# Down projections of a SwiGLU layer by seven products instead of eight, token differences on VectorE, h transposes one product later

## The chip, the cores and the metric

The kernel runs on one core of a Trainium2 chip. Its time is the device time of one execution in microseconds (us); lower is better. TensorE (PE) multiplies, VectorE (DVE), ScalarE (ACT) and GpSimd (POOL) work on vectors, and SyncE (SP) starts the transfers from HBM.

## The reference

One decoder layer in float32 for 256 tokens of width 2048. Each step works on an rms-normed x and is added to x:

```python
def swiglu(h, w_gate, w_up, w_down):
    return (jax.nn.silu(h @ w_gate) * (h @ w_up)) @ w_down

x = x + 0.5 * swiglu(rms_norm(x, ffn1_norm), ffn1_w_gate, ffn1_w_up, ffn1_w_down)
x = x + hybrid_mixer(...)        # attention and gated linear attention, 256 x 6160 and 2048 x 2048
x = x + cross_attention(...)     # 256 memory tokens, 4 heads of 128
x = x + 0.5 * swiglu(rms_norm(x, ffn2_norm), ffn2_w_gate, ffn2_w_up, ffn2_w_down)
```

w_gate and w_up are 2048 x 5632, w_down is 5632 x 2048. The change concerns the two ffns (swiglu) alone.

## The kernel before

**Precision.** Every f32 operand is split in two parts, hi and lo, and a product is three passes on TensorE: hi·wh, hi·wl, lo·wh. A weight tile `raw` (128 x 2048 f32, 512 rows of the weight by 512 columns, 1 MB) is loaded by SP's queue; `parts` cuts it in two halves, and for each ScalarE casts `wh` (L174) and VectorE subtracts `wl = raw - wh` (L175). wh and wl have four buffers each, so splitting can be four half tiles ahead of TensorE. `wgroup` does the same for ordinary projections (L127, L128).

**Stages of an ffn.** The 5632 hidden columns are 11 chunks f of 512, in two segments (0 to 5, 6 to 10). For each f the kernel computes gate and up (x times a 512-column chunk of w_gate and of w_up, accumulated over four groups of 512 rows of x), `silu` of gate on ScalarE (L366), times up on VectorE (L372, the rows `s<-s,r,sg`), which gives h for two token halves. The h chunk is transposed by TensorE (`turn`, four 128x128 transposes for each token half, L343) and split into `hTh` and `hTl` (L262 for the latter). After a segment, its h chunks are multiplied with w_down, 512 columns c at a time (c from 0 to 3), and x is updated (L379).

**Seven products.** For f > 0 `seven` computes gate and up of a chunk together. Its first two row groups make a 2 x 2 block problem: token half 1 and 2 of x by row group 1 and 2 (blocks A11, A12, A21, A22), row group by gate or up column (b11, b21, b12, b22). Seven block products stand for eight: weights are added (`add` on VectorE, L180, into b11 in place: b11+b21, then +b12, then +b22; a fourth sum on POOL's accumulating transfer, `add_hbm`), and x differences (`F`, five of them) take the place of x blocks. One block product (`product`) is 12 matmuls of 128x512 on a PSUM bank. The other row groups are ordinary (`plain`, 24 matmuls a tile). Four PSUM banks Y, Z, X, R hold the sums; Y is copied twice on ScalarE on the way (`s21`, `s22`) before it grows on. The products come in this order:

1. Y = A21·(b11+b21); ScalarE copies Y to s21
2. Z = F22-21·b21
3. Y += F12-21·(b11+b21+b12); ScalarE copies Y to s22
4. X = F22-12·b22
5. R = A12·(b11+b21+b12+b22)
6. Y += F21-11·b12; later the plain tiles, and last Y += F11-12·(b12+b11)

**Differences.** `differences()` runs once for each ffn, ahead of the first seven: four sums xf = xTh + xTl and five d on POOL, five `Fh` on ScalarE, five `Fl` on VectorE (L221). At the kernel's start POOL also makes the packed products of x and gain (L284) out of which xTh and xTl come.

**Order.** A scheduler sets the order on each engine from the order of the code and priorities: what stands in `tc.high_priority(WPRI)` (weights, their splits, `add`) goes ahead. `later(n, fn)` puts fn behind the n-th next `tick`, and every half tile of weights ticks once. So `later(1, ...)` puts the h transposes of one chunk near the middle of the first products of the next seven.

Of the kernel before, what the change touches and what calls it, by code (L numbers as in the profile page):

```python
# [38 lines left out]
XPRI = 170  # L39
MEM0 = 2  # L40
MEMS = 3
UB = 34
SB = 8
RB = 5
SEGS = (range(0, 6), range(6, NF))


@with_exitstack
def layer_kernel(ctx: ExitStack, tc: tile.TileContext, A: dict, out: bass.AP):
# [26 lines left out]
    def later(n, fn):  # L76
        pend.append([n, fn])
# [80 lines left out]

    def load(W, c, g):
        with tc.high_priority(WPRI):
            raw = wp.tile([P, 4, 512], F32, tag="raw", name="raw", bufs=RB)
            SY.dma_start(raw, W[c, g])
        return raw

    def parts(raw):
# [37 lines left out]
    def differences():  # L205

        x = {}
        for c in range(2):
            for t in range(TT):
                x[t, c] = U([P, 4, P], F32, "xf")  # L210
                hi, lo = (p[:, :, t * P:(t + 1) * P].bitcast(F32) for p in xT[c])
                G.tensor_tensor(x[t, c], hi, lo, op=ALU.add)
        r = {}
        for name, a, b in (("22-21", (1, 1), (1, 0)), ("12-21", (0, 1), (1, 0)), ("22-12", (1, 1), (0, 1)),
                           ("21-11", (1, 0), (0, 0)), ("11-12", (0, 0), (0, 1))):
            d = W2([P, 4, P], "d")
            G.tensor_tensor(d, x[a], x[b], op=ALU.subtract)
            hi = U([P, 4, P], F32R, "Fh")
            lo = U([P, 4, P], F32R, "Fl")
            SC.copy(hi, d)  # L220
            V.tensor_sub(lo, d, hi.bitcast(F32))  # L221
            r[name] = (hi, lo)
        return r

    def seven(W1, W2_, f, F, A12, A21, rest):


        Y, Z, X, R = [pa.tile([P, 512], F32, tag="acc", name="acc") for _ in range(4)]
        b11 = load(W1, f, 0)
        b21 = load(W1, f, 1)  # L230
        add(b11, b21)
        product(Y, A21, b11, True)
        s21 = W2([P, 512], "s21")
        SC.copy(s21, Y)
        b12 = load(W2_, f, 0)
# [5 lines left out]
        b22 = load(W2_, f, 1)  # L241
        product(X, F["22-12"], b22, True)
        add(b11, b22)
        product(R, A12, b11, True)
        V.tensor_sub(s22, R, s22)
        product(Y, F["21-11"], b12, False)
        add_hbm(b12, W1[f, 0])
        s12 = W2([P, 512], "s12")
        SC.copy(s12, Y)
        for g in (2, 3):  # L250
            plain((R, X), (rest(0, g), rest(1, g)), load(W2_, f, g), (False, False), (1, 0))
        V.tensor_sub(s12, R, s12)
        V.tensor_add(s22, X, s22)
        plain((Y, Z), (rest(0, 2), rest(1, 2)), load(W1, f, 2), (False, False), (1, 0))
        product(Y, F["11-12"], b12, False)
        plain((Y, Z), (rest(0, 3), rest(1, 3)), load(W1, f, 3), (False, False), (0, 1))
        V.tensor_add(s21, Z, s21)
        return Y, s21, s12, s22

    def split_from_psum(hi, lo, ps):  # L260
        SC.copy(hi, ps)
        V.tensor_sub(lo, ps, hi.bitcast(F32))  # L262
# [70 lines left out]
    def ffn(pre, r, after, fine=None, last=False):  # L333
        wg, wu, wd = (A[f"{pre}_w_{n}"] for n in ("gate", "up", "down"))
        hT = {}

        def turn(f, hs):
            for t in range(TT):
                hi = U([P, 4, P], F32R, "hTh")
                lo = U([P, 4, P], F32R, "hTl")  # L340
                tp = PM([P, 4, P], "tp")
                for j in range(4):
                    PE.transpose(tp[:, j], hs[t][:, j * P:(j + 1) * P], ident)  # L343
                split_from_psum(hi, lo, tp)
                hT[f, t] = (hi, lo)

        def x_block(t, c):
            return tuple(p[:, :, t * P:(t + 1) * P] for p in xT[c])

        def lhs_h(k, t):  # L350
            return tuple(p[:, k % 4] for p in hT[k // 4, t])

        for seg in SEGS:
            for f in seg:
                if f == 0:
                    acc = proj(wg, f, lhs_x, range(4), fine)
                    if callable(r):
                        r = r()
                    F = differences()
                else:  # L360
                    y, s21, s12, s22 = seven(wg, wu, f, F, x_block(0, 1), x_block(1, 0), x_block)
                    acc = [y, s21]
                sg = []
                for t in range(TT):
                    s = acc[t] if f and t else W2([P, 512], "sg")
                    SC.activation(s, acc[t], AF.Silu, scale=r[:, t:t + 1])  # L366
                    sg.append(s)
                acc = [s12, s22] if f else proj(wu, f, lhs_x, range(4))
                hs = []
                for t in range(TT):  # L370
                    h = acc[t] if f else W2([P, 512], "h")
                    V.scalar_tensor_tensor(h, acc[t], r[:, t:t + 1], sg[t], op0=ALU.mult, op1=ALU.mult)  # L372
                    hs.append(h)
                later(1, lambda f=f, hs=hs: turn(f, hs))
            final = seg is SEGS[-1]
            for c in range(NC):
                acc = proj(wd, c, lhs_h, seg, last=last and final and c == NC - 1)
                for t in range(TT):
                    V.scalar_tensor_tensor(xs[c][:, t], acc[t], 0.5, xs[c][:, t], op0=ALU.mult, op1=ALU.add)  # L379
                if final:  # L380
                    after(c)


    def head_scale(acc, r, r2, t, scale_in, sign, name):
# [18 lines left out]
        return r2  # L403


    mhalf = con.tile([P, P], F32, name="mhalf")
    V.memset(mhalf, -0.5)

    warm = ST(1, "warm")
    SC.activation(warm, mhalf[:, 0:1], AF.Silu)  # L410
    wps = PM([P, P], "wps")
    for i in range(WARM):
        PE.matmul(wps, mhalf, mhalf, start=True, stop=True)
    ident = con.tile([P, P], F32, name="ident")
    make_identity(nc, ident)

# [83 lines left out]
    q_turn = gated("q", 6)  # L500


    r2b = con.tile([P, TT, 32], F32, name="r2b")
    V.tensor_copy(r2b, r2.unsqueeze(2).broadcast_to([P, TT, 32]))
    gps = PM([32, S], "gps")
    for k in range(16):
# [500 lines left out]
```

## Time and profile before

| | |
|---|---|
| median of 3 runs | 1964.46 us (1963.1 to 1965.01) |
| the profiled execution | 1964.76 us, its span 1962.7 us |
| TensorE busy | 1933.6 us (99%) |
| VectorE busy | 1366.8 us (70%) |
| ScalarE busy | 1064.6 us (54%) |
| POOL busy | 110.6 us (6%) |
| granted TensorE clock, mean | 0.997 of full speed |
| HBM traffic | 395.24 MB, 201 GB/s |

In a row of groups, the columns are line, engine, operation, tiles (out<-in) with shapes and count, then busy us and mean ns, then idle time just before them and what ended it. In a timeline row they are start and duration in us, then the instruction, and in brackets the idle time ahead of it and its releaser. Matmuls overlap, so a matmul's duration is longer than the distance to the next; distances between starts tell the rate. PEld is the load of the stationary operand.

### The profile page before, as it was taken

Reading aid. Unit: us, or ns where it says so; the run is one execution under the profiler, and the core shown is the slowest. Engines: PE = TensorE matmul, PEld = TensorE weight load, DVE = VectorE, ACT = ScalarE, POOL = GpSimd, SP = SyncE. Lnnn points to the kernel's source line nnn. Section 1 sums busy time; section 2 is a strip of 40 time slices with the busy share of each in tenths; the row PEclk is TensorE's granted clock in tenths of the full one; section 3 lists DMA queues with packets and bytes.
Section 4 is the critical chain, followed back from the end, with each engine's and each line's share of the span. In section 5 each row is a group of like instructions: output and inputs, shape, how many; then the busy total and the mean of one; then the engine's idle time right before and its main releaser. Section 6 shows DMA issues by size and latency. Waiting matters only on the chain.

```text
span 1962.7 us, 22466 instructions
## 1 busy us (share of the span) xinstructions
PE 1933.6 (99%) x8760; PEld 1582.1 (81%) x8760; DVE 1366.8 (70%) x1388; ACT 1064.6 (54%) x1305; POOL 110.6 (6%) x99
## 2 busy tenths in 40 slices
PE   8899999999999999999999999999999999999999
PEld 6688788888778888878888889778778888877887
DVE  6788874578887554646775665878886457888643
ACT  5556653355665445544576545656665335666532
POOL 4100000000000000001221000300000000000000
PEclk9899999999999999999999999999999999999999
DMA  8466565556667554535466553556657555666652
GB/s 343 153 211 236 195 238 194 194 207 216 220 209 241 204 182 154 178 129 209 172 215 214 188 184 143 178 190 232 210 199 256 193 193 194 229 202 212 237 214 84
DMA packets 60566, 395.24 MB, mean 201 GB/s; under 512 B 6795, under 2 KB 7947, under 8 KB 14252
## 3 DMA queue, kind: packets, MB, share of 16 engines
q1 hardware_dynamic: 56428, 370.74, 51.6%
q0 software_dynamic: 2880, 20.97, 5.8%
q10 hardware_dynamic: 1152, 2.10, 0.3%
q8 instruction: 68, 1.11, 0.2%
q14 instruction: 38, 0.31, 0.0%
HBM read 391.69 MB, written 2.10 MB: 201 GB/s over the span
## 4 chain that ended last, share of the span: by engine, by line
PE 68%; DVE 20%; DMA 6%; issue 5%; ACT 1%; SPq 0%; DVEq 0%; ACTq 0%
PE acc L138 17%; PE acc L136 17%; PE acc L137 17%; DVE wl L175 13%; DMA raw<-in_ffn_w_gate_dram 6%; PE acc L191 5%; PE acc L190 5%; PE acc L189 5%; DVE raw L180 3%; DVE s L372 1%; ACT wh L174 1%; DVE hTl L262 1%; DVE wl L128 1%; PE tp L343 0%; PE tp L302 0%
## 5 line engine op out<-in xcount | busy, mean ns | idle before, releaser
L128 DVE TENSOR_TENSOR wl<-raw,wh 128x1024 fp32r<-128x1024 f32 (+1 forms) x370 | 459.4, 1246 | 367.8 <-ACT wh L127 365.4
L127 ACT CAST wh<-raw 128x1024 fp32r<-128x1024 f32 (+1 forms) x370 | 386.5, 1048 | 441.0 <-PE acc L138 400.6
L174 ACT CAST wh<-raw 128x1024 fp32r<-128x1024 f32 x440 | 457.8, 1053 | 308.8 <-PE acc L191 274.6
L175 DVE TENSOR_TENSOR wl<-raw,wh 128x1024 fp32r<-128x1024 f32 x440 | 522.2, 1223 | 94.1 <-ACT wh L174 91.0
L189 PE MATMUL acc<-wh,xTh 128*128 128x512 f32 x800 | 314.4, 393 | 3.5 <-ACT sg L366 2.3
L190 PE MATMUL acc<-wl,xTh 128*128 128x512 f32 x800 | 314.2, 393 | 1.5 <-DVE wl L175 0.8
L191 PE MATMUL acc<-wh,xTl 128*128 128x512 f32 x800 | 313.6, 392 | 0.0
L136 PE MATMUL acc<-wh,hTh 128*128 128x512 f32 x704 | 274.6, 390 | 0.0
L138 PE MATMUL acc<-wh,hTl 128*128 128x512 f32 x704 | 274.0, 389 | 0.0
L137 PE MATMUL acc<-wl,hTh 128*128 128x512 f32 x704 | 274.0, 389 | 0.0
L136 PE MATMUL acc<-wh,xTh 128*128 128x512 f32 x544 | 215.0, 396 | 5.4 <-ACT wh L127 2.8
L137 PE MATMUL acc<-wl,xTh 128*128 128x512 f32 x544 | 212.5, 391 | 2.6 <-DVE wl L128 2.6
L138 PE MATMUL acc<-wh,xTl 128*128 128x512 f32 x544 | 212.0, 390 | 0.7 <-DVE xTl L286 0.7
L189 PEld LDWEIGHTS acc<-wh,xTh 128*128 128x128 f32 x800 | 150.4, 188 | 42.3 <-ACT wh L174 9.3
L190 PEld LDWEIGHTS acc<-wl,xTh 128*128 128x128 f32 x800 | 150.4, 188 | 40.0 <-DVE wl L175 9.3
L191 PEld LDWEIGHTS acc<-wh,xTl 128*128 128x128 f32 x800 | 150.5, 188 | 30.3
L180 DVE TENSOR_TENSOR raw<-raw 128x2048 f32<-128x2048 f32 x60 | 137.3, 2289 | 51.2 <-DMA raw<-in_ffn_w_gate_dram 50.5
L191 PE MATMUL acc<-wh,Fl 128*128 128x512 f32 x400 | 157.0, 393 | 4.1 <-DVE Fl L221 4.1
L190 PE MATMUL acc<-wl,Fh 128*128 128x512 f32 x400 | 158.8, 397 | 0.2 <-DVE wl L175 0.2
L189 PE MATMUL acc<-wh,Fh 128*128 128x512 f32 x400 | 157.6, 394 | 0.0
L137 PEld LDWEIGHTS acc<-wl,hTh 128*128 128x128 f32 x704 | 132.2, 188 | 27.4
L138 PEld LDWEIGHTS acc<-wh,hTl 128*128 128x128 f32 x704 | 132.1, 188 | 27.3
(281 smaller groups left out, 1946.5 us busy)
## 6 DMA issues: line engine op xcount, KB each, us to landing
raw<-in_ffn_w_up_dram SPq DMA_DIRECT2D x88, 1024.0 KB, 4.8
raw<-in_ffn_w_down_dram SPq DMA_DIRECT2D x88, 1024.0 KB, 4.8
raw<-in_ffn_w_gate_dram SPq DMA_DIRECT2D x85, 1024.0 KB, 4.9
raw<-in_w_in_dram SPq DMA_DIRECT2D x48, 1024.0 KB, 4.8
raw<-in_ffn_w_gate_dram POOLq DMA_DIRECT2D x20, 1024.0 KB, 9.3
raw<-in_w_out_dram SPq DMA_DIRECT2D x16, 1024.0 KB, 4.8
raw<-in_xattn_w_k_dram SPq DMA_DIRECT2D x4, 1024.0 KB, 5.7
raw<-in_xattn_w_q_dram SPq DMA_DIRECT2D x4, 1024.0 KB, 4.8
```

What stands on the lines that cost most here:

```text
L127: SC.copy(wh[:, d], src)
L128: V.tensor_sub(wl[:, d], src, wh[:, d].bitcast(F32))
L136: PE.matmul(acc[t], lh, wh, start=first and i == 0, stop=False)
L137: PE.matmul(acc[t], lh, wl, start=False, stop=False)
L138: PE.matmul(acc[t], ll, wh, start=False, stop=last and i == len(half) - 1)
L174: SC.copy(wh, src)
L175: V.tensor_sub(wl, src, wh.bitcast(F32))
L180: V.tensor_add(dst, dst, src)
L189: PE.matmul(bank, hi[:, k], wh, start=start and i == 0, stop=False, skip_group_check=True)
L190: PE.matmul(bank, hi[:, k], wl, start=False, stop=False, skip_group_check=True)
L191: PE.matmul(bank, lo[:, k], wh, start=False, stop=stop and i == len(half) - 1, skip_group_check=True)
L262: V.tensor_sub(lo, ps, hi.bitcast(F32))
```

## The change

`seven` is generalised: a function `ld(col, k)` names the weight tile, `pair` the two row groups (or h chunks) that take part in the seven products, `others` the plain ones. It serves gate and up as before, with `pair` (0, 1), and now also down projections, for two column chunks c and c+1 at a time, with the first two h chunks of the segment as `pair`. A down seven so has seven products and plain tiles for the other four or three h chunks, its adds on VectorE and one more accumulating transfer on POOL's queue.

For that the h chunks of a pair need five differences too. `turn` keeps full copies `hf` of the pair's transposed chunks (ScalarE, L347), splits only the blocks that are used as they are, and when the pair's second chunk is there it makes five `d`, five `Fh`, five `Fl` by `difference` (d and Fl on VectorE, L215 and L218, Fh on ScalarE, L217, all at the priority of the weights). x differences are made by the same function, the four sums xf on VectorE too (L369); two of them are written over blocks of xT that nothing reads any more. POOL makes no differences any longer. The h transposes come at the second tick instead of the first (`TURN`), the x differences at the first and fifth tick behind the first gate chunk. The last down projection's special order (`last`) is gone, buffer counts change (UB, SB), and the warm-up matmuls read a tile of their own.

```diff
-UB = 34
-SB = 8
+UB = 36
+SB = 7
+DIFF = 1
+TURN = 2
...
+    def difference(x, name, home=None):
+        a, b = PAIRS[name]
+        with tc.high_priority(WPRI):
             d = W2([P, 4, P], "d")
-            G.tensor_tensor(d, x[a], x[b], op=ALU.subtract)
...
+            V.tensor_sub(d, x[a], x[b])
+            hi, lo = home or (U([P, 4, P], F32R, "Fh"), U([P, 4, P], F32R, "Fl"))
             SC.copy(hi, d)
             V.tensor_sub(lo, d, hi.bitcast(F32))
...
-    def seven(W1, W2_, f, F, A12, A21, rest):
+    def seven(ld, F, A12, A21, pair, others, rest):
+        k1, k2 = pair
         Y, Z, X, R = [pa.tile([P, 512], F32, tag="acc", name="acc") for _ in range(4)]
-        b11 = load(W1, f, 0)
-        b21 = load(W1, f, 1)
+        b11 = load(ld(0, k1))
+        b21 = load(ld(0, k2))
...
-        def turn(f, hs):
+        def turn(f, hs, pair):
             for t in range(TT):
...
+                if f in pair:
+                    j = pair.index(f)
+                    hf[t, j] = U([P, 4, P], F32, "hf")
+                    SC.copy(hf[t, j], tp)
+                    if t == j:
+                        continue
...
+            if f == pair[1]:
+                for name in PAIRS:
+                    FH[name] = difference(hf, name)
...
-                    F = differences()
+                    later(DIFF, lambda: x_differences(("22-21", "12-21", "22-12")))
+                    later(DIFF + 4, lambda: x_differences(("21-11", "11-12")))
...
-                later(1, lambda f=f, hs=hs: turn(f, hs))
+                later(TURN, lambda f=f, hs=hs, pair=pair: turn(f, hs, pair))
...
-            for c in range(NC):
-                acc = proj(wd, c, lhs_h, seg, last=last and final and c == NC - 1)
-                for t in range(TT):
-                    V.scalar_tensor_tensor(xs[c][:, t], acc[t], 0.5, xs[c][:, t], op0=ALU.mult, op1=ALU.add)
+            for c in range(0, NC, 2):
+                y, s21, s12, s22 = seven(lambda col, k: wd[c + col, k], FH, hT[pair[1], 0], hT[pair[0], 1], pair,
+                                         list(seg[2:]), lambda t, k: hT[k, t])
+                for d, acc in ((c, (y, s21)), (c + 1, (s12, s22))):
+                    for t in range(TT):
+                        V.scalar_tensor_tensor(xs[d][:, t], acc[t], 0.5, xs[d][:, t], op0=ALU.mult, op1=ALU.add)
```

What the scheduler makes of it is seen on VectorE. First the seven of f=2 in ffn1, after the second chunk of the pair. The `s` rows are the sums of the seven before and its product with r (h); `raw<-raw` is an add, `wl` a split. Before:

```order
L257 TENSOR_TENSOR s_566<-acc,s_566 128x512
L372 SCALAR_TENSOR_TENSOR s_678<-s_678,r_333,sg 128x512
L175 TENSOR_TENSOR wl<-raw,wh 128x1024 x2
L372 SCALAR_TENSOR_TENSOR s_611<-s_611,r_333,s_566 128x512
L175 TENSOR_TENSOR wl<-raw,wh 128x1024
L262 TENSOR_TENSOR hTl<-tp,hTh 128x512
L175 TENSOR_TENSOR wl<-raw,wh 128x1024
L180 TENSOR_TENSOR raw<-raw 128x2048
L175 TENSOR_TENSOR wl<-raw,wh 128x1024
L262 TENSOR_TENSOR hTl<-tp,hTh 128x512
L175 TENSOR_TENSOR wl<-raw,wh 128x1024 x8
```

Now, from the second product with r on (the rows ahead of it differ only in that three splits stand between the two):

```order
L399 SCALAR_TENSOR_TENSOR s_609<-s_609,r_335,s_564 128x512
L182 TENSOR_TENSOR raw<-raw 128x2048
L177 TENSOR_TENSOR wl<-raw,wh 128x1024 x2
L262 TENSOR_TENSOR hTl<-tp,hTh 128x512
L215 TENSOR_TENSOR d<-hf 128x512 x5
L218 TENSOR_TENSOR Fl<-d,Fh 128x512
L177 TENSOR_TENSOR wl<-raw,wh 128x1024
L218 TENSOR_TENSOR Fl<-d,Fh 128x512
L177 TENSOR_TENSOR wl<-raw,wh 128x1024
L218 TENSOR_TENSOR Fl<-d,Fh 128x512
```

The add (of b22) has moved ahead of hTl, and behind the two splits of b22 stand an hTl, five d and an Fl before the next split, which is that of the sum b11; the other Fl alternate with the splits that follow.

The second place is the middle of the first segment's down projections in ffn1 (x_105 is the first column chunk of x, x_106 the second). Before, where one column chunk follows the other, also on VectorE:

```order
L128 TENSOR_TENSOR wl<-raw,wh 128x1024 x10
L379 SCALAR_TENSOR_TENSOR x_105<-acc,x_105 128x512 x2
L128 TENSOR_TENSOR wl<-raw,wh 128x1024 x12
L379 SCALAR_TENSOR_TENSOR x_106<-acc,x_106 128x512 x2
L128 TENSOR_TENSOR wl<-raw,wh 128x1024 x12
```

Now, where the second column pair's seven follows the first's (s_2219 is s21 of the first):

```order
L182 TENSOR_TENSOR raw<-raw 128x2048
L177 TENSOR_TENSOR wl<-raw,wh 128x1024
L257 TENSOR_TENSOR s_2219<-acc,s_2219 128x512
L408 SCALAR_TENSOR_TENSOR x_105<-acc,x_105 128x512
L177 TENSOR_TENSOR wl<-raw,wh 128x1024 x3
L408 SCALAR_TENSOR_TENSOR x_105<-s_2219,x_105 128x512
L177 TENSOR_TENSOR wl<-raw,wh 128x1024 x2
L182 TENSOR_TENSOR raw<-raw 128x2048
L177 TENSOR_TENSOR wl<-raw,wh 128x1024 x8
```

Three adds have come into each down seven; the last of them (b22) stands here behind both splits of b22, and in the difference seven above it stands ahead of them.

The third place is the h transposes on TensorE, in the same seven of f=2 (xTh_134 and xTh_136 are the same block of x, A21). Before:

```order
L189 MATMUL acc<-wh,xTh_134 128x512
L190 MATMUL acc<-wl,xTh_134 128x512
L343 MATMUL tp<-ident,s_678 128x128 x4
L191 MATMUL acc<-wh,xTl_135 128x512
L189 MATMUL acc<-wh,xTh_134 128x512
L190 MATMUL acc<-wl,xTh_134 128x512
L191 MATMUL acc<-wh,xTl_135 128x512
```

Now:

```order
L191 MATMUL acc<-wh,xTh_136 128x512
L192 MATMUL acc<-wl,xTh_136 128x512
L193 MATMUL acc<-wh,xTl_137 128x512
L343 MATMUL tp<-ident,s_676 128x128 x4
L191 MATMUL acc<-wh,Fh 128x512
L192 MATMUL acc<-wl,Fh 128x512
```

The first four transposes stood four matmuls ahead of the end of the first product and stand now at its end; the second four move from the middle of the second product to its end. In the whole program 96 matmuls of 128x512 are gone.

More of the change, by code (lines that the diff above doesn't have):

```diff
@@ L234, in seven @@
         SC.copy(s21, Y)
-        b12 = load(W2_, f, 0)
+        b12 = load(ld(1, k1))
         product(Z, F["22-21"], b21, True)
@@ L335, in ffn @@
         hT = {}
-        def turn(f, hs):
+        F, FH = {}, {}
+        xf, hf = {}, {}
+        def turn(f, hs, pair):
             for t in range(TT):
-                hi = U([P, 4, P], F32R, "hTh")
-                lo = U([P, 4, P], F32R, "hTl")
                 tp = PM([P, 4, P], "tp")
@@ L353, in ffn @@
         for seg in SEGS:
+            pair = (seg[0], seg[1])
             for f in seg:
@@ L403, in squared @@
         return r2
-    mhalf = con.tile([P, P], F32, name="mhalf")
+    mhalf = con.tile([P, 8], F32, name="mhalf")
     V.memset(mhalf, -0.5)
+    idle = U([P, P], F32, "idle")
+    V.memset(idle, -0.5)
     warm = ST(1, "warm")
@@ L412, in layer_kernel @@
     for i in range(WARM):
-        PE.matmul(wps, mhalf, mhalf, start=True, stop=True)
+        PE.matmul(wps, idle, idle, start=True, stop=True)
     ident = con.tile([P, P], F32, name="ident")
```

54 lines of the change are left out of this document (30 added, 24 removed).

## The prediction

> **What bounds the kernel now.** I read the busy times first, then the clock row, the chain, the groups by line and the waits, and last the timelines of the stages that the change touches.
>
> ```profile
> PE 1933.6 (99%) x8760; PEld 1582.1 (81%) x8760; DVE 1366.8 (70%) x1388; ACT 1064.6 (54%) x1305; POOL 110.6 (6%) x99
> PE 68%; DVE 20%; DMA 6%; issue 5%; ACT 1%; SPq 0%; DVEq 0%; ACTq 0%
> DVE wl L175 <- ACT wh L174: 91.0, 55, 2.9
> PE tp L343 <- DVE s L372: 5.4, 8, 0.9
> ```
>
> TensorE (PE) is busy 99% of the span of 1962.7 us, so idle only 29.1 us: a removed matmul counts in full unless something new makes TensorE wait. The chain says who could: 20% of it runs through VectorE (DVE). The last row is the one wait that the old h transposes cause, eight times, 5.4 us in all. How near VectorE is to being the bound differs by stage (columns behind the comma: busy PE, PEld, DVE, ACT, POOL, then granted clock, DMA share, GB/s); the first of the two windows lies in gate-up sevens, the second in down projections:
>
> ```profile
> 200.00:250.00 50.00, 49.28 (x221) 39.72 (x220) 43.59 (x40) 31.21 (x36) 0.86 (x1) 1.00 0.62 210
> 300.00:350.00 50.00, 50.00 (x222) 41.43 (x221) 24.29 (x23) 19.16 (x19) 0.00 (x0) 1.00 0.56 198
> 316.70 1.28 DVE L379 SCALAR_TENSOR_TENSOR x<-acc,x 128x512 f32<-128x512 f32 x2
> 345.47 1.22 DVE L128 TENSOR_TENSOR wl<-raw,wh 128x1024 fp32r<-128x1024 f32 x1 [1.50 <-ACT wh L127]
> 349.34 1.28 DVE L379 SCALAR_TENSOR_TENSOR x<-acc,x 128x512 f32<-128x512 f32 x2
> ```
>
> VectorE works 43.59 of 50 us where sevens run and 24.29 where a down chunk does. Between the two x rows lies one down chunk of the first segment, 6 h chunks x 4 k-tiles x 3 passes x 2 token halves = 144 matmuls: 32.64 / 144 = 0.2267 us each, the pitch that all below uses. A product (12 matmuls) takes 2.72 us, a seven of gate and up (180 matmuls) 40.8. What it really takes is seen from its one subtraction into s21 (first and fifth row of a segment, and the last two of ffn2); the three rows behind are one of its two groups of four transposes:
>
> ```profile
> 112.46 0.68 DVE L257 TENSOR_TENSOR s<-acc,s 128x512 f32<-128x512 f32 x1
> 283.64 0.68 DVE L257 TENSOR_TENSOR s<-acc,s 128x512 f32<-128x512 f32 x1
> 1675.97 0.68 DVE L257 TENSOR_TENSOR s<-acc,s 128x512 f32<-128x512 f32 x1
> 1806.29 0.68 DVE L257 TENSOR_TENSOR s<-acc,s 128x512 f32<-128x512 f32 x1
> 1848.78 0.68 DVE L257 TENSOR_TENSOR s<-acc,s 128x512 f32<-128x512 f32 x1
> 504.46 0.60 PE L343 MATMUL tp<-ident,s 128*128 128x128 f32 x4
> 504.82 0.47 PE L190 MATMUL acc<-wl,Fh 128*128 128x512 f32 x1
> 505.13 0.39 PE L191 MATMUL acc<-wh,Fl 128*128 128x512 f32 x1
> ```
>
> Four sevens lie from 112.46 to 283.64 and from 1675.97 to 1848.78: 171.18 and 172.81 us, 43.0 each; the last of them, 42.49, is the shortest of all sixteen such periods. Four transposes cost 0.36 and slow the matmul behind them from 0.23 to 0.31: 0.9 for eight, so the seven's own work is 41.7. One seven, on VectorE:
>
> ```profile
> 496.64 2.29 DVE L180 TENSOR_TENSOR raw<-raw 128x2048 f32<-128x2048 f32 x1
> 498.85 1.22 DVE L175 TENSOR_TENSOR wl<-raw,wh 128x1024 fp32r<-128x1024 f32 x1
> 499.98 0.68 DVE L257 TENSOR_TENSOR s<-acc,s 128x512 f32<-128x512 f32 x1
> 500.58 0.74 DVE L372 SCALAR_TENSOR_TENSOR s<-s,r,sg 128x512 f32<-128x512 f32 x1
> 501.24 2.38 DVE L175 TENSOR_TENSOR wl<-raw,wh 128x1024 fp32r<-128x1024 f32 x2
> 505.34 0.68 DVE L262 TENSOR_TENSOR hTl<-tp,hTh 128x512 fp32r<-128x512 f32 x1
> 507.08 2.29 DVE L180 TENSOR_TENSOR raw<-raw 128x2048 f32<-128x2048 f32 x1
> 511.01 9.16 DVE L175 TENSOR_TENSOR wl<-raw,wh 128x1024 fp32r<-128x1024 f32 x8
> 520.09 0.68 DVE L245 TENSOR_TENSOR s<-acc,s 128x512 f32<-128x512 f32 x1
> 523.70 2.59 DVE L175 TENSOR_TENSOR wl<-raw,wh 128x1024 fp32r<-128x1024 f32 x2 [2.92 <-ACT wh L174]
> ```
>
> Four rows of the same kinds between them left out, VectorE has no gap from 496.64 to 520.77; then it idles 2.92 us behind a cast. Its pitches, from row to row: split of half a tile (wl) 1.14, add of two tiles (raw) 2.20, any 128x512 subtraction 0.60, product with r 0.66. Two splits cost 2.28 us and feed a product of 2.72, so VectorE keeps ahead by 0.44 us a product and loses it all at one add.
>
> **The change, part by part.**
>
> *Removed matmuls.* Each ffn has four down sevens (two column pairs, two segments), eight in all, each one product short: 96 matmuls x 0.2267 = **−21.8**. Weights loaded and split stay as many.
>
> *h transposes one product later.* Their wait on h (5.4 us above) goes, and hTl moves behind the third add on VectorE, so that the add comes 1.2 us sooner. Sixteen periods are concerned, 43.0 each. The floor is the own work, 41.7 (16 x 1.3 = −20.8); the waits alone give −5.4. I take the middle of 41.7 and of the shortest, 42.49, so 42.1: 16 x 0.9 = **−14.4**.
>
> *h differences.* In the second seven after each segment's pair (four sevens in all), VectorE gets five d and five Fl, less one hTl that is not split: 9 x 0.60 = 5.4 us, in the stretch above that has no gap. ScalarE gets five Fh. In the order they stand thus after the third add (2.20): two splits of b22 2.28, hTl 0.60, five d 3.00, one Fl 0.60, and only then the split that the fifth product waits for. The fifth product (R) needs it 4 x 2.72 + 0.9 of transposes = 11.8 us after the seven began; VectorE has by then s21 0.60, two products with r 1.32, three splits 3.42, the add 2.20, and the 6.48 just listed, and the split 1.14: 15.16, so 3.3 late. After that Fl and split alternate, 1.74 for each half product of 1.36, four times: 1.5 more. 4.8 a seven, x 4 = **+19.2**. Bounds: the idle 2.92 behind it absorbs its share, 5.4 − 2.92 = 2.5 each (+10); or ScalarE's turn makes it worse, 8.6 each (+34, the first rival).
>
> *Adds in down sevens, and in the seven after them.* No add stood in a down projection before. Where a seven follows a down seven, both splits of b22 stand ahead of the add of b22. From the end of the seven before: 0.60 + 0.66 + 3.42 + 0.66 + 2.28 + 2.20 = 9.82, then a cast and a split of the sum. For the cast:
>
> ```profile
> L174 ACT CAST wh<-raw 128x1024 fp32r<-128x1024 f32 x440 | 457.8, 1053 | 308.8 <-PE acc L191 274.6 <-PE acc L138 21.6 <-DVE raw L180 4.9
> ```
>
> 9.82 + 1.05 + 1.14 = 12.0 against the 10.9 (4 x 2.72) at which the fifth product wants it: 1.1 late. Where the add stands ahead of these splits, the cast and split run 2.28 sooner and it is 1.2 early. Five such places (second column pair in three segments, the gate-up seven after the first segment's downs in each ffn) 5.5; in the sixth, ffn1's last pair, norm's xg and xTl stand between, some 1.4 more: 2.5. Together **+8.0**; at nothing if buffers run ahead, +12 if each is 2. The eight more accumulate transfers on POOL's queue cost nothing: the row below has 9.3 us from issue to landing, and five to seven plain tiles (24 matmuls, 5.44 us each) stand between in a down seven. If one is late, the product with b12 at the end of a seven waits.
>
> ```profile
> raw<-in_ffn_w_gate_dram POOLq DMA_DIRECT2D x20, 1024.0 KB, 9.3
> ```
>
> *x differences.* POOL made them, beside VectorE:
>
> ```profile
> 19.43 7.90 POOL L212 TENSOR_TENSOR xf<-xTh,xTl 128x512 f32<-128x512 f32 x4
> 27.30 4.00 POOL L284 TENSOR_TENSOR xr<-xr,gain 128x512 f32<-128x512 f32 x2
> 23.88 6.51 DVE L128 TENSOR_TENSOR wl<-raw,wh 128x1024 fp32r<-128x1024 f32 x3
> 31.89 0.50 PE L138 MATMUL acc<-wh,xTl 128*128 128x512 f32 x1 [0.68 <-DVE xTl L286]
> 60.78 0.50 PE L189 MATMUL acc<-wh,xTh 128*128 128x512 f32 x1 [2.30 <-ACT sg L366]
> 73.86 0.79 PE L191 MATMUL acc<-wh,Fl 128*128 128x512 f32 x1 [4.14 <-DVE Fl L221]
> ```
>
> The last two products with gain wait 7.9 us behind four xf adds on POOL, and three splits take 6.51 where elsewhere they take 3.4. On VectorE the four adds cost 2.4, the splits win 3.1, and POOL's products end 5 or more sooner: the wait chain up to 31.89 ends about 3 sooner (1 to 4). Later the first product with r (h) stands behind five d, five Fl, four splits and an add: the two waits of 2.30 and 4.14 come back in another shape, 5 to 6 us ahead of the first transposes and a fifth product 1 to 2.5 late. Net −0.5, from −3.5 to +2.5. In ffn2 the differences fall in VectorE's idle time behind casts (1.50 in each 2.72 for weights taken singly, the row at 345.47), hence nothing; without that cover they would cost up to 5.4, as below.
>
> *Small edges.* The first column pair's down seven after a gate-up seven has the good order, about 0.25 each, four times +1.0; the tail gets a subtraction of 0.60 ahead of its last update. With −0.5: **+1.1**. Homes in xT, buffer counts and the idle tile move no work.
>
> Sum: −21.8 − 14.4 + 19.2 + 8.0 + 1.1 = −7.9. The profiled execution took 1964.76 us (0.30 above the median of the runs), so 1956.9.
>
> **The clock, by row and by rule.** The two waits last quoted were followed by half speed:
>
> ```profile
> 60.00:64.00 4.00, 3.22 (x11) 2.59 (x12) 4.00 (x4) 2.62 (x5) 0.00 (x0) 0.79 0.45 152
> 76.00:80.00 4.00, 4.00 (x12) 3.12 (x11) 1.60 (x3) 1.31 (x2) 0.00 (x0) 0.58 0.35 150
> 0.00:20.00 20.00, 15.13 (x63) 11.27 (x64) 11.06 (x15) 12.41 (x21) 7.39 (x14) 1.00 0.86 307
> 62.27 0.58 PE L189 MATMUL acc<-wh,xTh 128*128 128x512 f32 x1
> 65.64 0.44 PE L191 MATMUL acc<-wh,Fl 128*128 128x512 f32 x1
> ```
>
> Between the last two rows eight matmuls took 3.37 us, 0.42 each instead of 0.2267: 1.6 us lost after 2.30 us of waiting. Waits up to 1.31 us in the first 20 us left the clock at 1.00. A difference seven with one wait of 3.3 us may so lose 1.6 us more; I keep it out of the sum, since PE has work between the pieces, and put it into the rival. The Trainium skill's page "TensorE: Matmul & The Clock Gate", Part 1, states that the clock halves after an idle window of about 3.4 us in a free-running count; by it waits of 3.3 us or less would hardly ever drop it and the first rival's time would be 1964.1 and not 1972. The row at 62.27, half speed after 2.30 us, does not bear that out as a lower limit.
>
> **The rivals.**
>
> *Slower: the difference sevens tangle.* Place: the four sevens above. ScalarE's five Fh stand in its queue between casts that wait for TensorE, and the copies of Y (s21, s22) stand behind them, on which the third and sixth products wait. By hand along both queues the fourth product waits 2.5, the third 1.6, the sixth 2.5: 6.6 a seven, and one drop of the clock of about 2.0: 8.6. 4 x (8.6 − 4.8) = +15.2: 1972.1. It decides from 7.8 a seven on (7.9 + 3.9 = 11.8 over four, above 4.8). For it: VectorE's gapless 24 us and the half speed after 2.30. Against: ScalarE is busy 31 of 50 us there, and it has never been what TensorE waited for in a seven.
>
> *Faster: the differences hide.* 2.5 a seven, as bounded: −9.2, 1947.7. For it: idle of 2.92 behind casts in each seven, 91.0 us over all of them. Against: that idle lies behind the product that needs the splits.
>
> *No change: the transposes' wait only moves.* VectorE, not the place of the transposes, is what the product phase waits for; then only 5.4 comes of that term: −21.8 − 5.4 + 19.2 + 8.0 + 1.1 = +1.1, 1965.9. For it: VectorE without gap up to 520. Against: the shortest periods, 42.49, are those without that wait.
>
> **How the numbers follow.** About 0.2% (3.9 us) is what a measurement of this kernel can tell from no change. Forecast 0.34, 1951 to 1962, nine tenths of it faster; tangle 0.24, most of it slower; hidden 0.20, faster; no change 0.22. Faster 0.31 + 0.20 = 0.51; same 0.03 + 0.18 + 0.03 = 0.24; slower 0.21 + 0.04 = 0.25. The range goes from the hidden case, 1947, to a little beyond the tangle, 1974; what is left out at both ends (all terms at their floor, or the clock dropping twice) I hold for less than 2 in 10.
>
> **What would show it.** TensorE with 96 instructions fewer. No wait of the h transposes on the product with r. Four places with TensorE waits of 2 to 4 us, one in the seven after each second chunk of a segment, released by VectorE's splits; if released by ScalarE's copies s21 and s22, with a clock slice below 9, the tangle. Six waits of about 1 us at the first matmul of R after a down seven. Periods of other sevens near 42.1; if 42.7 and more, the third rival. The wait at 31.9 some 3 us sooner, and 5 to 6 us of idle ahead of the first transposes of ffn1. The prediction is wrong if the order's rows are not how the engines meet: if VectorE is far ahead when a difference seven begins, or if a down seven waits for its raw tiles.

## The result, and the profile after

The changed kernel took 1997.96 us (median of 4 runs, 1996.64 to 1999.76), the kernel before 1964.74 beside it: 1.0174 times as long, 95% interval 1.0161 to 1.0187. The forecast was 1956.9, faster, with a range up to 1974. The change is 33 us slower: the other way than forecast, and above the range. The profiled execution of the changed kernel took 1996.64 us (span 1994.5, against 1962.7).

The page of the changed kernel, busy times and clock:

```profile
PE 1924.2 (96%) x8664; PEld 1573.4 (79%) x8664; DVE 1505.2 (75%) x1543; ACT 1139.1 (57%) x1405; POOL 84.6 (4%) x89
PEclk9899999999999999999999999999999999999999
```

The 96 matmuls are gone (8664 instructions, 8760 before), but TensorE is now idle 70.3 us (1994.5 − 1924.2) instead of 29.1, and the clock, 0.997 on the mean before, is 0.991. The clock row in tenths is digit for digit that of before: drops of some 3.4 us, shown below, do not appear in slices of 50 us. TensorE's waits, by what released them (total us, times, longest; one row of 0.2 left out):

```profile
PE acc L192 <- DVE wl L177: 25.7, 20, 2.4
PE acc L191 <- ACT s L232: 7.7, 5, 2.1
PE acc L138 <- ACT wh L129: 6.4, 1, 6.4
PE acc L191 <- ACT s L238: 6.2, 5, 1.4
PE tp L343 <- DVE h L399: 5.3, 1, 5.3
PE acc L191 <- ACT sg L393: 5.2, 1, 5.2
PE acc L191 <- ACT wh L176: 3.3, 9, 0.5
PE acc L138 <- DVE x L945: 3.2, 1, 3.2
PE tp L343 <- DVE s L399: 1.4, 2, 0.7
```

The wait of the transposes on h shrank from 5.4 to 1.4 us, as the edit does. Everything above it is new or larger: splits that come late (L177), and ScalarE's two copies of Y (L232 and L238), on which TensorE never waited before. (The 6.4 us lie at the very start, where the warm-up matmuls stood before.)

Where they lie is seen from the distances between the s21 subtractions, one for each seven:

```profile
115.04 0.68 DVE L257 TENSOR_TENSOR s<-acc,s 128x512 f32<-128x512 f32 x1
163.73 0.68 DVE L257 TENSOR_TENSOR s<-acc,s 128x512 f32<-128x512 f32 x1
206.94 0.68 DVE L257 TENSOR_TENSOR s<-acc,s 128x512 f32<-128x512 f32 x1
```

The first stood at 112.46 before: the start lost 2.6. The seven that ends at 163.73 is a difference seven, that is one in which the h differences are made: 48.7; the next, an ordinary one, 43.2. From all such rows, after minus before, the 31.8 us of span come together so (the forecast's own terms for the same stretch beside it):

| stretch | forecast | measured |
|---|---|---|
| start, up to the first s21 | −0.5 | +2.6 |
| 16 periods in four groups, of these four difference sevens 48.69, 50.18, 51.56, 50.29 (before 43.0 each) | +4.8 | +30.9 |
| down projections of the first segments and the seven after, twice | −6.0 | −3.1 |
| ffn1's last down projections, mixer, up to ffn2's first s21 | −2.7 | +4.5 |
| ffn2's last down projections and the end | −3.5 | −3.1 |

In the second row the four difference sevens make +28.7, the twelve ordinary periods +2.3 (mean 43.2, not 42.1).

A difference seven on VectorE (first six rows), ScalarE (next three) and TensorE (last three), in the changed kernel's timeline:

```profile
120.47 2.29 DVE L182 TENSOR_TENSOR raw<-raw 128x2048 f32<-128x2048 f32 x1
122.67 2.35 DVE L177 TENSOR_TENSOR wl<-raw,wh 128x1024 fp32r<-128x1024 f32 x2
124.94 0.68 DVE L262 TENSOR_TENSOR hTl<-tp,hTh 128x512 fp32r<-128x512 f32 x1
125.54 3.09 DVE L215 TENSOR_TENSOR d<-hf 128x512 f32<-128x512 f32 x5
128.55 0.68 DVE L218 TENSOR_TENSOR Fl<-d,Fh 128x512 fp32r<-128x512 f32 x1
129.15 1.22 DVE L177 TENSOR_TENSOR wl<-raw,wh 128x1024 fp32r<-128x1024 f32 x1
126.39 0.61 ACT L217 CAST Fh<-d 128x512 fp32r<-128x512 f32 x1
126.90 1.04 ACT L176 CAST wh<-raw 128x1024 fp32r<-128x1024 f32 x1
127.85 0.57 ACT L232 COPY s<-acc 128x512 f32<-128x512 f32 x1
123.94 0.50 PE L192 MATMUL acc<-wl,Fh 128*128 128x512 f32 x1 [2.39 <-DVE wl L177]
128.47 0.50 PE L191 MATMUL acc<-wh,Fh 128*128 128x512 f32 x1 [1.44 <-ACT s L232]
136.16 0.50 PE L191 MATMUL acc<-wh,xTh 128*128 128x512 f32 x1 [1.44 <-ACT s L238]
```

TensorE waits first for a split of b22, which stands behind the add that was moved ahead (120.47), then for the copy of Y, which stands behind a Fh and a cast in ScalarE's queue, then for the second copy: 2.39, 1.44, 1.44. TensorE takes the fourth product ahead of the third here, so these are waits of the fourth, the third and the sixth product. That is the tangle that the first rival worked out along both queues (2.5, 1.6 and 2.5), not the wait of 3.3 at the fifth product that the sum was made of. In three of the four the clock dropped besides, in the longest of them twice; the first two rows are from the second and the fourth, the last from the first, which kept its clock (windows of the changed kernel, TensorE's clock behind POOL's column):

```profile
528.00:532.00 4.00, 3.62 (x9) 2.88 (x10) 3.31 (x4) 1.01 (x2) 0.86 (x1) 0.57 0.66 125
1767.00:1771.00 4.00, 4.00 (x11) 3.15 (x12) 3.33 (x4) 1.04 (x1) 0.75 (x1) 0.57 0.68 107
120.00:124.00 4.00, 1.58 (x9) 0.84 (x8) 4.00 (x4) 2.08 (x3) 0.00 (x0) 1.00 0.41 172
```

An ordinary seven shows a wait that no part of the prediction named:

```profile
236.20 2.29 DVE L182 TENSOR_TENSOR raw<-raw 128x2048 f32<-128x2048 f32 x1 [4.34 <-DMA raw<-in_ffn_w_gate_dram]
238.41 3.49 DVE L177 TENSOR_TENSOR wl<-raw,wh 128x1024 fp32r<-128x1024 f32 x3
239.68 0.50 PE L192 MATMUL acc<-wl,xTh 128*128 128x512 f32 x1 [1.79 <-DVE wl L177]
```

VectorE stands idle for 4.34 us ahead of the first add of the next seven, waiting for its transfer, and the split that TensorE needs for the present plain tile is behind it. There are nine such waits of 0.42 to 1.79 us, 9.9 of the 25.7 us that TensorE waits for these splits.

### The profile page after: what moved, and what is told of

The parts are those of the page before. It is cut to its first block, busy times and chain, and to the rows that moved or that the text cites. A ratio compares the mean times of both kernels' runs of the same rounds, so it can differ in the third digit from the quotient of the medians.

```text
span 1994.5 us, 22580 instructions
## 1 busy us (share of the span) xinstructions
PE 1924.2 (96%) x8664; PEld 1573.4 (79%) x8664; DVE 1505.2 (75%) x1543; ACT 1139.1 (57%) x1405; POOL 84.6 (4%) x89
## 5 line engine op out<-in xcount | busy, mean ns | idle before, releaser
L176 ACT CAST wh<-raw 128x1024 fp32r<-128x1024 f32 x664 | 697.2, 1054 | 557.0 <-PE acc L193 471.2
L177 DVE TENSOR_TENSOR wl<-raw,wh 128x1024 fp32r<-128x1024 f32 x664 | 787.4, 1220 | 188.1 <-ACT wh L176 181.2
L192 PE MATMUL acc<-wl,xTh 128*128 128x512 f32 x960 | 378.1, 394 | 11.7 <-DVE wl L177 11.5
L130 DVE TENSOR_TENSOR wl<-raw,wh 128x1024 fp32r<-128x1024 f32 (+1 forms) x194 | 237.0, 1227 | 151.6 <-ACT wh L129 151.0
L129 ACT CAST wh<-raw 128x1024 fp32r<-128x1024 f32 (+1 forms) x194 | 201.5, 1043 | 182.6 <-PE acc L140 162.2
L191 PEld LDWEIGHTS acc<-wh,xTh 128*128 128x128 f32 x960 | 181.8, 189 | 56.6 <-ACT s L238 7.0
L139 PE MATMUL acc<-wl,xTh 128*128 128x512 f32 x544 | 214.2, 394 | 0.0
L193 PEld LDWEIGHTS acc<-wh,xTl 128*128 128x128 f32 x960 | 182.0, 190 | 38.0
L192 PE MATMUL acc<-wl,hTh 128*128 128x512 f32 x512 | 199.9, 390 | 3.1 <-DVE wl L177 3.0
L191 PE MATMUL acc<-wh,hTh 128*128 128x512 f32 x512 | 199.6, 390 | 1.4 <-ACT wh L176 1.4
L193 PE MATMUL acc<-wh,hTl 128*128 128x512 f32 x512 | 199.4, 389 | 0.0
L138 PEld LDWEIGHTS acc<-wh,xTh 128*128 128x128 f32 x544 | 103.1, 189 | 32.2 <-ACT wh L129 6.8
L140 PEld LDWEIGHTS acc<-wh,xTl 128*128 128x128 f32 x544 | 103.3, 190 | 21.8
```

What stands on the lines that cost most here:

```text
L129: SC.copy(wh[:, d], src)
L130: V.tensor_sub(wl[:, d], src, wh[:, d].bitcast(F32))
L138: PE.matmul(acc[t], lh, wh, start=first and i == 0, stop=False)
L139: PE.matmul(acc[t], lh, wl, start=False, stop=False)
L140: PE.matmul(acc[t], ll, wh, start=False, stop=last and i == len(half) - 1)
L176: SC.copy(wh, src)
```

## The experiments

Each is an edit of the changed kernel unless said; "1998" is the changed kernel.

**The place of the h differences.**

```diff
-                for name in PAIRS:
-                    FH[name] = difference(hf, name)
+                def make(name):
+                    FH[name] = difference(hf, name)
+                for i, name in enumerate(PAIRS):
+                    later(11 + 2 * i, lambda name=name: make(name))
```

> The changed kernel (1998.0), but the five h differences of a segment are made one by one at five later ticks of the same seven (from its last products through its plain tiles) instead of all at once behind the transposes. Theory A (their place in VectorE's and ScalarE's queues makes the four sevens after each second chunk 48.7 to 51.6 us long, against 43.3 of the others): these four periods come to 43 to 44.5, 1998 - 4 x 6.5 = 1972 (1967 to 1978). Rival (the 5.4 us of VectorE's extra work is paid wherever it stands): the periods stay above 48, 1990 or more.

1980.32 us (1.0088 of before, 1.0073 to 1.0103). The periods came to 45.84, 48.19, 47.05 and 45.34: better, not free. One wait remained in each, 3.13 us, released by VectorE's subtraction `R - s22`, which has no priority and so stood behind the differences. Hence the same once more from the tenth tick on and with `pri=0`:

> The changed kernel (1998.0); the five h differences are made one at a time from the tenth tick on and without the weights' priority, so that they stand behind the subtraction R - s22 and among the splits of the plain tiles. In the spread version those periods were still 45.3 to 48.2, with one wait of 3.1 us for that subtraction. Theory A (place in the queue is all of the cost): the four periods come to 43 to 44, 1998 - 26 = 1972 (1968 to 1976). Rival (VectorE has no room in the plain tiles either, since the adds wait there for transfers): 45 and more, 1978 to 1985.

1975.57 us (1.0058, 1.0041 to 1.0075). Periods 44.96, 44.50, 44.59, 46.09; no wait on the copies of Y is left in them, and the waits on the subtraction are gone. Of the 28.7 us above 43.0 are left 8.1; the rest was the place in the queues and not the work, for VectorE's instructions are as many. Theory A holds for the larger part. Some 2 us a seven stay, as the rival would have it, but none of them was tested singly; what the trace shows is VectorE coming late to the h behind these sevens, on which the transposes now wait more (1.4 us in the changed kernel):

```profile
PE tp L343 <- DVE s L402: 6.4, 7, 1.2
```

**The transposes.**

> The changed kernel with the h transposes at the first tick again. Theory B (with late transposes the order lets the first add of the next seven, which waits for its transfer, stand one split further ahead, so TensorE waits 0.6 to 1.8 us at the last plain tile of an ordinary seven; the early transposes take that back): the twelve ordinary periods go from 43.3 to 43.0 and the wait of the transposes on h comes back, 1994 (1990 to 1998). Rival (late transposes are a gain that something else hides): 2003 to 2010.

1993.53 us (1.0150, 1.0133 to 1.0167), as theory B expected: ordinary periods 42.9 on the mean, the waits on h back at 5.7 us, those on splits down from 25.7 to 10.0. The interval just overlaps that of the changed kernel; the rows are the better evidence, for the nine waits behind a waiting add are gone. The difference sevens still took 49.6 to 50.9, with other waits, so their tangle does not come from the add that the late transposes moved ahead. The same from the other side, in the kernel before:

```diff
-                later(1, lambda f=f, hs=hs: turn(f, hs))
+                later(2, lambda f=f, hs=hs: turn(f, hs))
```

> The kernel before with the h transposes at the second tick and nothing else changed. Theory B (late transposes free VectorE earlier in the seven, and the order then puts the first add of the next seven, which waits for its transfer, one split further ahead): the waits on h (5.4 us) go, waits of 0.5 to 1.8 us on a split come at the third plain tile of ordinary sevens, sixteen periods 43.0 to 43.4, 1964.5 to 1970. The prediction's term: sixteen periods of 42.1, 1950. Rival in between: only the 5.4 us go, 1959.

1960.13 us beside 1961.98: 0.9992, 0.9983 to 1.0001, so no difference that can be told, where the prediction's term was −14.4. The waits on h are gone from the table of that kernel's waits, and this row has grown instead (1.0 us, twice, in the kernel before):

```profile
PE acc L190 <- DVE wl L175: 11.6, 13, 1.6
```

The wait moved, as the third rival had it, but not to the product phase: these waits lie in the plain tiles, behind the next seven's first add. The last seven of each segment, which no seven follows, has no such add behind it. With late transposes it took 41.9 us in all four places (42.5 in the kernel before), near the 42.1 of the forecast; the other twelve stayed at 43.3 on the mean (43.2). The last one, from its two s21 rows in this run:

```profile
1800.41 0.69 DVE L257 TENSOR_TENSOR s<-acc,s 128x512 f32<-128x512 f32 x1
1842.29 0.68 DVE L257 TENSOR_TENSOR s<-acc,s 128x512 f32<-128x512 f32 x1
```

**Down projections by eight products again**, no h differences; the rest of the change stays.

> The changed kernel with the down projections by eight products as before, without h differences; late transposes, x differences on VectorE, the late warm-up and the buffer counts stay. Theory A and B with the start (115.0 instead of 112.5 at the first seven's end): before + 2.6 + 16 x 0.3 = 1964.5 + 7.4, about 1972 (1968 to 1976). Rival (the ordinary sevens are long only because of the down sevens and difference tiles around them): periods of 42.1 to 42.5, 1955 to 1961.

1967.29 us (1.0022, 1.0013 to 1.0032). Between the two expectations, nearer the first: the late transposes, the x differences and the late warm-up alone cost some 4 us, and the down sevens with their differences cost the other 30. The forecast's terms for them were −21.8 for the removed matmuls, +19.2 for the h differences, +8.0 for the adds and +1.6 for the edges: 7.0 slower already.

**The add of b22 ahead of its splits.**

```diff
+        add(b11, b22)
         product(X, F["22-12"], b22, True)
-        add(b11, b22)
```

> The changed kernel with the add of b22 written ahead of the product that splits b22, in all sevens. Theory C (where a seven follows a down seven, the add stands behind two splits of b22 and R waits 1.27 us): these waits go at five places (6.4 us) and shrink at the sixth, 1991 (1988 to 1994). Rival (the add then waits for b22's transfer and holds the splits back everywhere): 1998 to 2010.

1991.40 us (1.0144, 1.0129 to 1.0159): 6.6 less, as expected. The places behind a down seven went from waits of 0.51 + 0.76 to at most 0.8, the gate-up seven after the first down projections in ffn2 from 44.01 to 42.47. The five places had waits of 6.2 us together in the changed kernel, and their periods got 4.6 shorter: that term of the prediction, 5.5, was about right.

**The norm of ffn1's first two column chunks** at ticks 13 and 15 of the last down seven instead of 1.

> The changed kernel, with the normalised transposes of the first two column chunks of ffn1's last segment put into the plain tiles of the last down seven (ticks 13 and 15) instead of its first product. Theory D (the ten vector instructions of norm in the product phase are what makes that seven wait 1.6, 0.8, 2.1 and 0.5 us and drop the clock): its waits go, 1991 (1989 to 1994). Rival (they are due to the add behind the splits alone): 1996 to 1998.

1988.33 us (1.0127, 1.0112 to 1.0142), 9.6 less. The s21 rows of that pair, in this run:

```profile
696.67 0.68 DVE L257 TENSOR_TENSOR s<-acc,s 128x512 f32<-128x512 f32 x1
750.38 0.68 DVE L257 TENSOR_TENSOR s<-acc,s 128x512 f32<-128x512 f32 x1
```

53.7 where it was 61.9 (697.59 to 759.45). In the changed kernel norm's rows stood in the product phase, and TensorE waited for splits and for the copy of Y (VectorE, then TensorE):

```profile
707.46 1.28 DVE L304 TENSOR_TENSOR xg<-tp,gain 128x512 f32<-128x512 f32 x2
706.46 0.50 PE L192 MATMUL acc<-wl,Fh 128*128 128x512 f32 x1 [1.60 <-DVE wl L177]
715.59 0.50 PE L191 MATMUL acc<-wh,Fh 128*128 128x512 f32 x1 [2.14 <-ACT s L232]
```

**x differences on POOL as before.**

> The changed kernel with the x differences' sums and subtractions on POOL as before (homes and ticks stay). Theory E (on VectorE they put the square root of the norm and the first h behind them, which makes the two waits of 5.2 and 5.3 us at the start of ffn1): the first s21 comes at 112 to 113 instead of 115.0, and nothing is lost in ffn2: 1995 (1993 to 1997). Rival (POOL slows VectorE's splits in the first 30 us again): 1998 to 2001.

1994.38 us (1.0154, 1.0139 to 1.0169). The time is as expected (its interval overlaps that of the changed kernel) and the reason was not: the first s21 came at 116.4, later than 115.0, with waits of 4.6 and 6.5 us at ffn1's start. What was won lies ahead of ffn2 (588.9 us from ffn1's last s21 to ffn2's first, against 591.9). There the changed kernel has, on VectorE and TensorE:

```profile
1258.31 1.29 DVE L369 TENSOR_TENSOR xf<-xTh,xTl 128x512 f32<-128x512 f32 x2
1260.65 2.48 DVE L945 TENSOR_TENSOR x<-acc,x 128x512 f32<-128x512 f32 x4
1261.48 0.47 PE L138 MATMUL acc<-wh,xTh 128*128 128x512 f32 x1 [3.23 <-DVE x L945]
```

The sums xf, at the weights' priority, went ahead of the adds that free the PSUM banks. "In ffn2 the differences fall in VectorE's idle time" was wrong by this.

**The warm-up.** In the changed kernel these matmuls run at 17.5 us, since the tile that they read is set behind twelve rows of VectorE, and the first real matmuls run at half speed, 0.43 us from start to start:

```profile
17.50 2.50 PE L445 MATMUL wps<-idle 128*128 128x128 f32 x20 [0.16 <-DVE idle L439]
11.02 0.63 PE L138 MATMUL acc<-wh,xTh 128*128 128x512 f32 x1
11.45 0.63 PE L139 MATMUL acc<-wl,xTh 128*128 128x512 f32 x1
```

> The changed kernel with the warm-up matmuls on a small tile that is set first, so that they run before the first weights arrive and not at 17.5 us, behind two transfers. Theory F (half speed up to 13 us costs nothing, since the transfers set the pace there, and the late warm-up costs its own 2.5 us at most): first s21 at 113 to 115, 1996 (1994 to 1998). Rival (the late warm-up is what lengthened the start): first s21 at 110 to 112, 1992 to 1994.

1997.81 us (1.0175, 1.0156 to 1.0195): nothing. The reason expected, that the transfers set the pace, is not what the rows show. With the early warm-up the first gate and up chunk (192 matmuls) began its last matmul at 54.8 us instead of 56.1, but the wait for silu behind it grew from 5.2 to 6.8 us: what was won went into that wait.

**All that helped together**, and x differences without priority, the first three already in the first gate projection, the sums of squares ahead of the casts:

```diff
+                    later(6, lambda: x_differences(("22-21", "12-21", "22-12")))
                     acc = proj(wg, f, lhs_x, range(4), fine)
...
+            with tc.high_priority(300):
+                sumsq(c, xs[c], ss1)
+        with tc.high_priority(400):
+            return rstd_of(ss1, "r1")
```

> The changed kernel with all that helped alone, transposes at the second tick: h differences among the plain tiles without priority, the add of b22 ahead of its splits, the norm of ffn1's first two column chunks in the plain tiles, and x differences without priority, the first three already during the first gate projection, the sums of squares ahead of the casts. From 1975.6: 9.6 less for norm, 6.6 for the add, 3 for the wait on x ahead of ffn2, 3 to 6 for the start: 1952 (1947 to 1958). If the removed products cannot be had because VectorE is the limit in down sevens too: 1962 or more.

> The same as the run with all that helped, but with the transposes at the first tick. Theory B: the ordinary sevens lose the waits behind the early add and get back those on h: within 3 us of the other, rather 2 less, 1950. If late transposes are a gain: 4 to 8 us more.

1951.66 us (0.9944, 0.9930 to 0.9957) with late transposes, 1947.49 us (0.9927, 0.9914 to 0.9941) with early ones: both faster than both kernels, the first by the sum expected, the second 2.5 lower. The 4.2 us between the two are more than the 2 expected, but their intervals overlap. The start gave more than was thought: in the second of them the first s21 stands at 105.5 (112.5 before). From that run's page and timeline:

```profile
PE 1909.4 (98%) x8664; PEld 1565.0 (80%) x8664; DVE 1503.8 (77%) x1543; ACT 1140.1 (59%) x1405; POOL 85.3 (4%) x89
105.48 0.69 DVE L257 TENSOR_TENSOR s<-acc,s 128x512 f32<-128x512 f32 x1
24.79 1.29 DVE L215 TENSOR_TENSOR d<-xf 128x512 f32<-128x512 f32 x2
```

**The same with eight products**, so that the start and the down sevens can be told apart:

> The fastest version (transposes at the first tick, 1947.5) with the down projections by eight products again and without h differences; the x differences early, the sums of squares ahead and the add of b22 ahead of its splits stay. It tells how much of the 14.5 us below the kernel before is the down sevens and how much the start. By the rows of that version the down sevens save 10.5 us of down time (pairs of 64.2, 63.6, 53.3, 53.7 instead of 65.3 and 54.4) and cost 7.7 in the four sevens with h differences (44.9, 44.5, 44.6, 45.7 against 43.0): 1950 to 1951. If the removed products are worth their 21.8 us: 1969. If they are worth nothing: 1945 to 1948.

1950.84 us (0.9938, 0.9924 to 0.9951), as the rows said. So of the 14.5 us by which the fastest version is below the kernel before, some 12 come from the start, the way into ffn2 and the order. The down sevens bring 3.3 by the medians and 2.2 by the ratios, which the two overlapping intervals can't tell from nothing. Stretch by stretch, the version with down sevens against this one: the two stretches from the last gate-up s21 to that of the seven after the downs are 169.7 and 170.5 us against 173.1 and 173.1, from ffn1's last gate-up s21 to ffn2's first 694.3 against 698.9, the end 110.4 against 114.0: 14.3 saved of the 21.8 removed. The four groups of sevens with h differences are 174.2, 173.2, 173.2 and 174.7 against 170.7, 171.2, 170.7 and 171.6: 11.0 given back. Most of that is seen as transposes waiting for h, 13.7 us against 4.5; the four longest, 1.85 to 2.48, stand right behind the sevens in which the differences are made. Of the 7.5 us lost in the down sevens, 0.9 each, one wait is seen in the timeline, 0.76 us at the first matmul of R, for the cast of the summed weights; the rest was not settled.

## Why the prediction was wrong, point by point

- *Removed matmuls, −21.8*: right in number; they are gone from every down seven. In time, the fastest version saved 14.3 of them.
- *Transposes, −14.4*: the step that failed most, some 17 of the 40 us between forecast and result. It took the middle between the own work and the shortest period, as if VectorE's lead would turn into TensorE's time. Alone it measured −1.5 over the sixteen periods, within the noise of the time (before with late transposes), and in the changed kernel the twelve ordinary periods got 0.2 longer. When hTl goes back, the adds come one split earlier, the first add of the next seven too, and that one waits for a transfer. The prediction followed the add of b22 and not the one behind it. Two splits stood ahead of the waiting add before (first two rows); one stands ahead of it now (last row, the split ahead of the add at 236.20 above):

```profile
221.55 2.58 DVE L175 TENSOR_TENSOR wl<-raw,wh 128x1024 fp32r<-128x1024 f32 x2 [2.94 <-ACT wh L174]
227.44 2.29 DVE L180 TENSOR_TENSOR raw<-raw 128x2048 f32<-128x2048 f32 x1 [3.30 <-DMA raw<-in_ffn_w_gate_dram]
230.63 1.22 DVE L177 TENSOR_TENSOR wl<-raw,wh 128x1024 fp32r<-128x1024 f32 x1 [2.87 <-ACT wh L176]
```

The argument against the third rival was a misreading as well: that the shortest periods, 42.49, are those without the wait on h. The wait stands in that very period (1806.29 to 1848.78, before), and one stands in the last period of each of the other three groups. These four are short though they have the wait; what sets them apart is that no seven follows them.

```profile
1807.78 0.63 PE L343 MATMUL tp<-ident,s 128*128 128x128 f32 x4 [0.85 <-DVE s L372]
```

- *h differences, +19.2*: that they delay the difference sevens was right; the place of the waits and the size were not. Above a base of 42.1 they were put at 4.8 a seven; measured are 48.7 − 43.2 = 5.5 where the clock held, 7.0 with one drop and 8.4 with two. The step added only VectorE's delay at the fifth product; the waits came at the fourth, third and sixth, two of the three through ScalarE's copies. The rival that followed both queues had 6.6 and one drop of the clock. Against it stood that ScalarE "has never been what TensorE waited for in a seven"; the row at 60.78 that the prediction shows, 2.30 us for ScalarE's silu at a seven's first product, says otherwise. It "decides from 7.8 a seven on" stood against the other terms as forecast, and these had failed too.
- *Adds, five places, 5.5*: about right, waits of 6.2 us, of which 4.6 went with the add moved ahead.
- *The sixth place, 2.5*: 8.2 by its period, 9.6 by the time. Norm's instructions were priced as "1.4 more" on VectorE; they are a difference seven in small, with the same wait on the copy of Y (2.14) and a clock drop.
- *x differences, −0.5*: +2.6 at the start and about +3 ahead of ffn2. What stood for the loss was seen (5 to 6 us ahead of the transposes; measured 5.3), but netted against a gain of 3 at the first waits, of which 2 came. The root of the norm came later too:

```profile
52.07 0.15 DVE L322 TENSOR_REDUCE r1t<-ss 128x2 f32<-128x8 f32 x1
59.44 0.15 DVE L322 TENSOR_REDUCE r1t<-ss 128x2 f32<-128x8 f32 x1
```

(before, then after; the changed kernel's matmuls are 2 us ahead there and silu still 0.95 later). That the idle tile moves no work was false as well: the warm-up moved, and setting that right gained nothing.
- *The clock*: kept out of the sum because "PE has work between the pieces". Rows show half speed of some 3.4 us in three of four difference sevens, behind waits of 1.4 to 2.4 us, some 1.6 us each time. The rule of the Trainium skill's page "TensorE: Matmul & The Clock Gate", Part 1 (half speed after an idle window of about 3.4 us), would have left these sevens at full speed, since no wait in them is that long; the window of 528 to 532 us, 0.57, disagrees.

The range failed because it let only the h differences vary, from hidden to tangled, and took the other terms as forecast. But the transposes, the x differences and norm's place all came out dearer, and the mechanisms of two rivals were at work at once. With the first rival's 8.6 a seven and the third's 5.4 the prediction's own sum is −21.8 − 5.4 + 34.4 + 8.0 + 1.1 = +16.3, or 1981, already above the range. The forecast's gain hung on the transposes alone: without that term the sum is 6.5 us slower. In the difference sevens, at norm's place and behind the waiting adds it was VectorE or ScalarE, with other work ahead in its queue, that held TensorE up.

## What to carry to other kernels

Where an engine has no gap, work added to its queue is paid at its place. The same work some 10 to 20 us later, where VectorE has gaps, cost little more than a quarter (8.1 us instead of 28.7): look at the place before counting the work. A copy or an add that waits must be followed with all that stands behind it in its queue, on the second engine too. Look at what an edit drags along (priority, tiles, the next add): a wait removed at one place came back at the next in both kernels in which it was tried.

## What the runs showed that was not expected

The same wait of 2.39 us on a split left the clock at 1.00 in three difference sevens (one is the row of 120 to 124 us) and was followed by half speed in another (1360.20; 0.42 us a matmul up to 1364), and waits of 1.44 us by half speed at 528.4 and 1766.9 but not at 136.2. The first difference seven had the same three waits with the add of b22 ahead of its splits (2.38, 1.27, 1.44), yet it took 51.6 us there and 48.7 in the changed kernel. In the first 20 us, waits of 1.31 and 1.02 us left the clock at 1.00 in the kernel before (16 to 20 us), and waits of 1.31 and 1.03 with the early warm-up were followed by 0.63. In these rows the drop lasts some 3.4 us and does not follow from the length of one wait. Taking the h differences out of the product phase also raised the mean clock, from 0.991 to 0.994, and with all edits to 0.997.
